# Moving two of ScalarE's four rows in each middle tile to VectorE, in a row normalization

## Chip, cores, metric

The kernel runs on one core of a Trainium2 chip. Times are device microseconds (us). A run is timed several times in turn with the kernel before on the same chip. The span of a profile, from the first to the last instruction, is some 1.7 us shorter than the time.

## The reference

```python
# x: float32, 32 x 512 x 1024
sums = np.sum(np.abs(x), axis=-1, keepdims=True)
return (x / (sums + 1e-8)).astype(np.float32)
```

There are 16384 rows of 1024 numbers. Each is read once and written once, 67.1 MB each way.

## The kernel before

Each of the 128 partitions holds 128 rows, cut into ten tiles of 12 rows and a last one of 8. A tile is loaded by SyncE's queue, reduced on VectorE, scaled in place by VectorE (the first `kv` rows, one instruction) and by ScalarE (the other rows, one instruction each), and stored from ScalarE's queue. Four tile buffers go round: the load of a tile waits until the store four tiles earlier has landed.

```python
R = 12; BUFS = 4
# ...
def normalize(x_tile, r0, k, kv):
    # s = sum |x| by row (line 51), s += EPS (58), inv = 1/s (60), all on VectorE
    nc.vector.tensor_mul(out=x_tile[:, r0:r0+kv, :], in0=x_tile[:, r0:r0+kv, :],     # line 61
                         in1=inv[:, :kv].unsqueeze(2).to_broadcast([P, kv, d]))
    for r in range(kv, k):                                                           # line 68
        nc.scalar.activation(out=row, in_=row, func=Copy, scale=inv[:, r:r+1])
# ...
for i, k in enumerate(rows):
    nc.sync.dma_start(out=x_tile[:, :k, :], in_=piece(x_flat, i))                    # line 78
    normalize(x_tile, 0, k, k - k // 3 - (i == 0))
    nc.scalar.dma_start(out=piece(out_flat, i), in_=x_tile[:, :k, :])                # line 81
```

(The excerpt is tightened; some lines and arguments are cut.)

## Time and profile before

| quantity | before |
|---|---|
| time, median of 3 runs | 317.16 us (316.67 to 318.14) |
| VectorE / ScalarE busy | 234.7 us (74%) / 47.2 us (15%) |
| moved by DMA | 134.2 MB, 425 GB/s over the span |
| share of the 16 DMA engines | load queue 49.8%, store queue 49.1% |
| VectorE waiting for loads | 59.8 us, of which 17.7 us for the first |

### The profile page before, as it was taken

How to read it: one execution, taken by the hardware profiler on the slowest of the kernel's cores; microseconds unless marked ns; L12 is line 12 of the kernel's file. 1: busy time of each engine (PE TensorE's matmuls, PEld its weight loads, DVE VectorE, ACT ScalarE, POOL GpSimd, SP SyncE). 2: the span in 40 equal slices, each digit the busy share in tenths (PEclk: the TensorE clock that was granted, in tenths of full speed). 3: DMA queues.
4: the chain of work that ended last, by engine and by line, in shares of the span. 5: the costliest groups of instructions: out<-in, count | busy, mean ns of one | idle time of the engine just before them, and what ended most of it. 6: DMA issues, size and time to landing. Idle time of an engine off the chain costs nothing.

```text
span 315.5 us, 206 instructions
## 1 busy us (share of the span) xinstructions
DVE 234.7 (74%) x44; ACT 47.2 (15%) x44; POOL 0.2 (0%) x4
## 2 busy tenths in 40 slices
DVE  0079999999999399929955992899199659979500
ACT  0010603105005001300500050013004000502000
POOL 0000000000000000000000000000000000000000
DMA  8999999999999999999999999999999999999996
GB/s 330 467 399 430 467 343 455 399 467 430 399 467 430 399 486 411 405 486 405 424 474 399 436 461 399 467 430 399 467 425 405 474 403 459 407 472 411 424 432 274
DMA packets 3169, 134.23 MB, mean 425 GB/s; under 512 B 352, under 2 KB 352, under 8 KB 352
## 3 DMA queue, kind: packets, MB, share of 16 engines
q1 hardware_dynamic: 1584, 67.11, 49.8%
q10 hardware_dynamic: 1584, 67.11, 49.1%
q14 instruction: 1, 0.01, 0.0%
HBM read 67.11 MB, written 67.11 MB: 425 GB/s over the span
## 4 chain that ended last, share of the span: by engine, by line
another core or an unknown queue 36%; DMA 31%; DVE 26%; SPq 0%; issue 0%; DVEq 0%; ACTq 0%
DMA x_tile<-in_x_dram 16%; DMA out_dram<-x_tile 15%; DVE s L51 15%; DVE x_tile L61 10%; SPq L78 0%; DVE inv L60 0%; DVE s L58 0%; DVEq L60 0%; ACTq L81 0%
## 5 line engine op out<-in xcount | busy, mean ns | idle before, releaser
L51 DVE TENSOR_REDUCE s<-x_tile 128x12 f32<-128x12288 f32 (+1 forms) x11 | 138.2, 12563 | 59.8 <-DMA x_tile<-in_x_dram 59.8
L61 DVE TENSOR_TENSOR x_tile<-x_tile,inv 128x8192 f32<-128x8192 f32 (+2 forms) x11 | 92.4, 8401 | 0.4
L68 ACT ACTIVATE x_tile<-x_tile,inv 128x1024 f32<-128x1024 f32 x43 | 45.9, 1136 | 226.9 <-DVE inv L60 226.9
L68 ACT ACT_TABLE_LOAD x1 | 1.3, 1283 | 17.7 <-DMA x_tile<-in_x_dram 17.7
L60 DVE RECIPROCAL inv<-s 128x12 f32<-128x12 f32 (+1 forms) x11 | 2.5, 226 | 0.9
L58 DVE TENSOR_SCALAR s<-s 128x12 f32<-128x12 f32 (+1 forms) x11 | 1.9, 173 | 0.4
L96 POOL MEMSET const-bfloat16-1.0<- 128x1 bf16 x1 | 0.1, 102 | 0.0
L96 POOL MEMSET const-uint8-127<- 128x1 uint8 x1 | 0.1, 102 | 0.0
L96 POOL MEMSET const-float32-0.0<- 128x1 f32 x1 | 0.1, 99 | 0.2 <-issue 0.2
L96 POOL MEMSET const-float32-1.0<- 128x1 f32 x1 | 0.1, 99 | 0.0
## 6 DMA issues: line engine op xcount, KB each, us to landing
x_tile<-in_x_dram SPq DMA_DIRECT2D x10, 6144.0 KB, 37.6
out_dram<-x_tile ACTq DMA_DIRECT2D x10, 6144.0 KB, 50.7
x_tile<-in_x_dram SPq DMA_DIRECT2D x1, 4096.0 KB, 32.3
out_dram<-x_tile ACTq DMA_DIRECT2D x1, 4096.0 KB, 18.2
```

The source lines that it names most:

```text
L51: nc.vector.tensor_reduce(out=s[:, :k], in_=x_tile[:, r0 : r0 + k, :], axis=mybir.AxisListType.X, op=mybir.AluOpType.add, apply_absolute_v ...
L58: nc.vector.tensor_scalar_add(out=s[:, :k], in0=s[:, :k], scalar1=EPS)
L60: nc.vector.reciprocal(out=inv[:, :k], in_=s[:, :k])
L61: nc.vector.tensor_mul(out=x_tile[:, r0 : r0 + kv, :], in0=x_tile[:, r0 : r0 + kv, :], in1=inv[:, :kv].unsqueeze(2).to_broadcast([P, kv, d]),)
L68: nc.scalar.activation(out=row, in_=row, func=mybir.ActivationFunctionType.Copy, scale=inv[:, r : r + 1],)
L96: nc = _bacc.Bacc("TRN2", target_bir_lowering=False, num_devices=1)
```

## The change

The intent is to divide the scaling differently: two rows of each tile on ScalarE, five of the first one, the others on VectorE.

```diff
-            normalize(x_tile, 0, k, k - k // 3 - (i == 0))
+            normalize(x_tile, 0, k, k - (2 if i else 5))
```

## The prediction

> **What bounds the kernel now.** I read the page first, then the chain that ended last, then the groups with their shapes kept apart, then the timeline, and last a table of stretches. The page's busy lines and its DMA lines:
>
> ```profile
> DVE 234.7 (74%) x44; ACT 47.2 (15%) x44; POOL 0.2 (0%) x4
> ...
> DVE  0079999999999399929955992899199659979500
> ...
> DMA  8999999999999999999999999999999999999996
> ```
>
> VectorE is busy 74% of the span, but the DMA row is at 9 from the second slice to the last but one: the 16 DMA engines never stop. Whoever has spare time, it is not they. The stretches from one load's landing to the next say how close to full they are (columns: stretch and its length, VectorE, ScalarE and GpSimd busy, TensorE clock, DMA share, GB/s):
>
> ```profile
> 111.17:140.20 29.03, 22.05 (x4) 4.26 (x4) 0.00 (x0) 1.00 1.00 433
> 140.20:169.18 28.98, 22.05 (x5) 4.26 (x4) 0.00 (x0) 1.00 1.00 434
> 169.18:198.19 29.01, 22.04 (x4) 4.26 (x4) 0.00 (x0) 1.00 1.00 434
> ```
>
> One tile of 12 rows takes 29.0 us at a DMA share of 1.00, and VectorE works 22.05 us of it. So VectorE has about 6.9 us to spare in each tile. The timeline shows that spare time as a wait for the load, in brackets:
>
> ```profile
> 96.23 8.69 DVE L61 TENSOR_TENSOR x_tile<-x_tile,inv 128x8192 f32<-128x8192 f32 x1
> ...
> 105.00 0.34 ACTq L81 DMA_DIRECT2D out_dram<-x_tile  x1
> 111.17 12.95 DVE L51 TENSOR_REDUCE s<-x_tile 128x12 f32<-128x12288 f32 x1 [6.26 <-DMA x_tile<-in_x_dram]
> ...
> 124.71 4.26 ACT L68 ACTIVATE x_tile<-x_tile,inv 128x1024 f32<-128x1024 f32 x4 [24.21 <-DVE inv L60]
> 124.71 8.69 DVE L61 TENSOR_TENSOR x_tile<-x_tile,inv 128x8192 f32<-128x8192 f32 x1
> 133.49 0.34 ACTq L81 DMA_DIRECT2D out_dram<-x_tile  x1
> ```
>
> The reader is to see that both halves of a scaling start together at 124.71, that ScalarE is done after 4.26 us and VectorE after 8.69, and that the store goes out when VectorE ends. ScalarE's end decides nothing, while VectorE's end is the moment at which a store is issued. Whether that moment matters is told by the chain of the work that ended last:
>
> ```profile
> 82.95 48.50 DMA out_dram<-x_tile
> 131.44 0.02 issue
> ...
> 131.52 0.33 SPq L78
> 131.85 28.65 another core or an unknown queue
> ...
> 248.08 32.26 DMA x_tile<-in_x_dram
> 280.34 0.02 issue
> 280.36 8.70 DVE s L51
> ```
>
> A load is issued when the store of the tile that held its buffer (four tiles earlier) has landed: the store issued at 82.95 lands at 131.44, and the load follows at 131.52. The store took 48.5 us, yet two transfers of 6.29 MB, in and out, fill only 29.0 us. The rest is queueing behind the store before it. That backlog is what the prediction rests on.
>
> **What the Trainium skill says.** (1) "DMA: Bandwidth & Descriptors", section "Where 436 GB/s comes from", gives a fabric ceiling of 435.2 GB/s. The trace agrees: 433 to 434 GB/s in the middle. (2) The same page, "Queues, rings and completion order", says that each DMA engine takes turns packet by packet between the queues that have work. So while loads and stores both have work queued, neither the order nor the speed depends on when a transfer was put in its queue. The trace agrees as far as it goes: equal bytes each way at 29.0 us a tile. [...] (4) "SBUF — State Buffer", section "Who interferes with whom", says that DMA has ports of its own and does not contend with compute engines. The trace lends it no more than weak support: in the tail 417 GB/s were moved while VectorE worked (280.4 to 296.2) and 416 just after it had stopped (296.3 to 304.8).
>
> **The change, part by part.** The first tile keeps 5 rows on ScalarE and 7 on VectorE (before it was 12/3 + 1 = 5 as well). The last tile of 8 rows keeps 2 and 6. Only the nine tiles between change, from 4 rows on ScalarE and 8 on VectorE to 2 and 10. The order of instructions on each engine is otherwise the same, with 18 activations fewer. The rates come from the groups by shape:
>
> ```profile
> L61 DVE TENSOR_TENSOR x_tile<-x_tile,inv 128x8192 f32<-128x8192 f32 x9 | 78.2, 8693 | 0.3
> ...
> L61 DVE TENSOR_TENSOR x_tile<-x_tile,inv 128x6144 f32<-128x6144 f32 x1 | 6.6, 6558 | 0.0
> ```
>
> - VectorE: two rows, 2048 elements, cost 8693 − 6558 = 2135 ns. The product of 10 rows should take 8693 + 2135 = 10828 ns[...]. Nine of them add 19.2 us: busy 234.7 → 253.9 us, 80% of the span.
> - ScalarE: four rows took 4.26 us and the last tile's two took 2.19, so a tile loses 2.07 us, nine lose 18.6: busy 47.2 → 28.6 us, 9%. It was done 4.4 us before VectorE and will be 8.6 us before it; nothing waits for either.
> - In a middle tile: VectorE 22.05 + 2.14 = 24.2 us against 29.0. The wait for the load shrinks from about 6.8 to about 4.6 us, and stores are issued some 2.1 to 2.3 us later. No new sum is on the path unless the store queue runs dry.
> - In the opening, where VectorE runs four tiles without a wait, delays add up: the second tile's store 2.1 us later, the third's 4.3, the fourth's 6.4 (105.00 → 111.4). The fifth tile's load lands at 111.17, so VectorE takes it about 0.2 us late, and the 6.26 us wait is gone. From there the delay falls back to 2.1 to 2.3.
> - Does the store queue run dry? The first store lands just before 73.52, when SyncE issues the fifth load, and the second store was issued at 60.9: 12.6 us to spare, of which 2.1 go. The third was issued at 82.95, and the second lands at about 102.5 (the sixth load goes out at 102.58): 19.6, of which 4.3 go. The fourth was issued at 105.00 and the third lands at 131.44: 26.4, of which 6.4 go. Later ones have about 27 us, of which 2.3 go. It never runs dry, so each store should land when it did, each load be issued when it was, and each tile arrive when it did.
> - In the tail: the last load lands at 280.34. The ninth changed tile is reduced from 256.18 on; its product should end at 278.40 + 2.14 = 280.54. The last tile's reduce then starts 0.2 us late, and its store is issued at about 296.4 instead of 296.24. Page part 6 has for that store
>
> ```profile
> out_dram<-x_tile ACTq DMA_DIRECT2D x1, 4096.0 KB, 18.2
> ```
>
> and 4.19 MB at 425 GB/s need only 9.9 us. So 8.3 us of backlog lie before it, and 0.2 us of delay is hidden. It should land in 18.0 us instead of 18.2, at the same 314.4.
>
> The sum: 19.2 us of VectorE work added, 18.6 us of ScalarE work removed, on the path 0.0 us. Prediction 317.2 us.
>
> **The rivals.** (a) VectorE becomes the bound. It would need over 29.0 us a tile, and it has 24.2. The opening is the only place where it sets the pace; if those 6.4 us counted in full, the time would be 323.6 (+2.0%). Against it stand the 12 to 26 us of backlog. (b) The later store delays the buffer, so the next load. The chain speaks for it, as loads are issued on stores' landings. If a landing moved with its issue, each lap of four tiles would add about 2.1 us, two to three laps 4 to 6 us: 321 to 323. Against it: a store waits behind others for 10 to 27 us before its own bytes move. (c) DMA moves more slowly while VectorE reads and writes on-chip memory. In stretches where VectorE is idle I find 469 GB/s against 431 during a reduce and 457 during a product. If that is real, 19.2 us more at 457 than at 469 cost about 0.5 us. The stretches always fall on the same phase of a tile and packets are counted whole, so I think little of it; the tail's 417 and 416 speak against. (d) A gain. Fewer instructions stand ahead of the store issue on ScalarE, but the issue waits for VectorE anyway. I find nothing that comes earlier.
>
> **Range and chances.** The three runs of before span 316.67 to 318.14, which is 0.5%; my central case adds nothing, so that scatter is most of the range: 316.3 to 318.5, the upper side a little wider for (c). To be slower by over 2% (323.5) takes (a) or (b) in full, which the backlog excludes unless I misread it: 0.02. Faster by over 2% would mean over 6 us less at a DMA share that is already 1.00: 0.005. Within 2%: 0.975.
>
> **What would show it.** Right: ten-row products of 10.83 us, VectorE at about 254 us and ScalarE near 29; waits of the reduce for a load down from 59.8 to about 41 us in total (17.7 at the start, none at the fifth tile and the last, about 4.6 at the five between); tiles still arriving at 140.2, 169.2, 198.2 and so on at 29.0 us; the last store landing in about 18.0 us. Step by step wrong: if tiles arrive later by 2 us a lap, (b) is right and the backlog was not there; if the fifth tile's load lands 6 us later, (a); if the arrivals are 29.1 us or more apart at a share of 1.00, (c).

## The result

The changed kernel took 317.20 us (median of 6 runs, 316.65 to 317.51), the kernel before 317.32 us in the 6 runs that it has by then. The ratio is 0.9993, with a 95% interval from 0.9975 to 1.001. A ratio here is the mean time of one kernel's fast runs over that of the other's of the same rounds, so it isn't quite the ratio of the medians quoted. Executions over 1.5% slower than the fastest of the same kernel are left out of the means.

The profile page after, its busy lines and DMA line:

```profile
DVE 253.8 (80%) x44; ACT 28.5 (9%) x26; POOL 0.2 (0%) x4
...
DVE  0079999999999999949985995899499959999500
...
DMA  8999999999999999999999999999999999999996
```

VectorE gained 19.1 us and ScalarE lost 18.7, while the DMA row has the same digits as before. The stretches from one tile's reduce to the next (columns as in the prediction):

```profile
111.44:140.46 29.02, 24.18 (x4) 2.19 (x2) 0.00 (x0) 1.00 1.00 434
140.46:169.44 28.98, 24.18 (x4) 2.19 (x2) 0.00 (x0) 1.00 1.00 434
169.44:198.47 29.03, 24.18 (x4) 2.19 (x2) 0.00 (x0) 1.00 1.00 433
```

A tile still takes 29.0 us, with VectorE busy 24.18 us of it instead of 22.05. The timeline shows where the extra 2.13 us went:

```profile
111.44 12.95 DVE L51 TENSOR_REDUCE s<-x_tile 128x12 f32<-128x12288 f32 x1
111.48 0.34 ACTq L81 DMA_DIRECT2D out_dram<-x_tile  x1
...
124.97 10.82 DVE L61 TENSOR_TENSOR x_tile<-x_tile,inv 128x10240 f32<-128x10240 f32 x1
...
135.89 0.34 ACTq L81 DMA_DIRECT2D out_dram<-x_tile  x1
140.46 12.95 DVE L51 TENSOR_REDUCE s<-x_tile 128x12 f32<-128x12288 f32 x1 [4.66 <-DMA x_tile<-in_x_dram]
```

The fourth store is issued at 111.48 instead of 105.00, and VectorE no longer waits for the fifth tile. One tile on, the wait is 4.66 us where it was 6.80. The extra work has been taken out of a wait. The chain that ended last, which now runs through other pieces:

```profile
111.48 49.11 DMA out_dram<-x_tile
160.59 0.02 issue
...
218.67 37.75 DMA x_tile<-in_x_dram
256.42 0.02 issue
256.44 12.96 DVE s L51
...
280.79 8.61 DVE s L51
```

The fourth store was issued 6.5 us later and lands at 160.59; in the kernel before it landed at 160.50, as the load waiting for it shows. That is the backlog at work. VectorE's share of the chain rose from 26% to 42%. In part this is because the last tile's reduce now starts when VectorE is free (280.71), 0.1 us after its load landed (280.60), where before it started at 280.36 on the landing at 280.34: two nearly equal predecessors changed places. For the rest, the chain now runs through the fourth store, issued at 111.48, and no longer through the third, at 82.95, so more of VectorE's opening lies on it. The time did not move. A share of the chain is thus not a measure of what an engine costs.

### The profile page after: what moved, and what is told of

It reads as the page before. It is cut to its first block, busy times and chain, and to the rows that moved or that the text cites. A ratio compares the mean times of both kernels' runs of the same rounds, so it can differ in the third digit from the quotient of the medians.

```text
span 315.7 us, 188 instructions
## 1 busy us (share of the span) xinstructions
DVE 253.8 (80%) x44; ACT 28.5 (9%) x26; POOL 0.2 (0%) x4
## 4 chain that ended last, share of the span: by engine, by line
DVE 42%; DMA 33%; another core or an unknown queue 18%; issue 0%; SPq 0%; DVEq 0%; ACTq 0%
DVE s L51 23%; DVE x_tile L61 18%; DMA x_tile<-in_x_dram 17%; DMA out_dram<-x_tile 16%; DVE inv L60 0%; DVE s L58 0%; SPq L78 0%; DVEq L60 0%; ACTq L81 0%
## 5 line engine op out<-in xcount | busy, mean ns | idle before, releaser
L61 DVE TENSOR_TENSOR x_tile<-x_tile,inv 128x10240 f32<-128x10240 f32 (+2 forms) x11 | 111.6, 10146 | 0.4
L68 ACT ACTIVATE x_tile<-x_tile,inv 128x1024 f32<-128x1024 f32 x25 | 27.2, 1139 | 245.9 <-DVE inv L60 245.9
```

Source lines behind the costliest of these rows:

```text
L61: nc.vector.tensor_mul(out=x_tile[:, r0 : r0 + kv, :], in0=x_tile[:, r0 : r0 + kv, :], in1=inv[:, :kv].unsqueeze(2).to_broadcast([P, kv, d]),)
L68: nc.scalar.activation(out=row, in_=row, func=mybir.ActivationFunctionType.Copy, scale=inv[:, r : r + 1],)
```

## The experiments

Eleven runs were made, in three groups; each group shared its runs of the kernel before, whose median in them was 316.9 to 317.0 us. The theory under test is the backlog: a store issued later still lands at the same time as long as the store queue has work, so nothing behind it moves. The time from a store's issue to the landing of the store in front of it is called its reserve: a delay up to that long is hidden. The rivals are that the delay passes on with the buffers, that DMA slows beside a busy VectorE, and, for the later runs, that only VectorE's pace against 29.0 us counts.

### all_vector: ScalarE scales nothing in the middle tiles

```diff
-            normalize(x_tile, 0, k, k - (2 if i else 5))
+            normalize(x_tile, 0, k, k - ((5, 0)[i > 0] if i < len(rows) - 1 else 2))
```

> VectorE scales all 12 rows of the nine middle tiles, ScalarE none there (first and last tile as before). VectorE then takes 22.05 + 4 x 1.07 = 26.3 us a middle tile against 29.0 of the DMA. Backlog theory (a store is issued later but waits behind earlier stores anyway, so its landing does not move): stores two to four are issued 4.3, 8.5 and 12.8 us later than in the kernel before, against 12.6, 19.6 and 26.4 us to spare; the last store is issued near 298.9, the store ahead of it lands near 304.9, so the time stays at 317.2 (within 0.3%). Rival 'delay passes on' (each lap of the four buffers inherits VectorE's delay): 4.3 us in each of two to three laps, 326 to 330. Rival 'DMA slows beside VectorE': 38 us more VectorE work, 1 us or more, 318.2 upward, with tiles arriving over 29.05 us apart.

Measured: 316.69 us, ratio 0.9975 (0.9928 to 1.0023). VectorE was busy 272.8 us (87%), and tiles arrived at 111.1, 140.1 and 169.1, again 29.0 us apart. Both rivals named so far fall here: 38 us more VectorE work than in the kernel before slowed no transfer, and twice the delay of the change reached nothing. The last store was issued at 298.24 and took 15.6 us to land, against 18.2: the delay is paid out of queueing.

### after_x4, before_x4, after_x8: more VectorE work

An extra reduce into scrap, from rows that are there anyway, in each of the nine middle tiles. It stands ahead of the product, so the store waits for it. The same edit on the kernel before gives before_x4, and 8 rows in place of 4 give after_x8.

```diff
+        if extra:
+            scrap = stats.tile([P, R], FP32)
+            nc.vector.tensor_reduce(out=scrap[:, :extra], in_=x_tile[:, r0 : r0 + extra, :], ...)
...
-            normalize(x_tile, 0, k, k - (2 if i else 5))
+            normalize(x_tile, 0, k, k - (2 if i else 5), 4 if 0 < i < len(rows) - 1 else 0)
```

> The changed kernel, with an extra reduce of 4 rows into scrap on VectorE in each of the nine middle tiles (4096 x 1.042 + 153 ns = 4.42 us), output unchanged. VectorE takes 24.2 + 4.4 = 28.65 us a tile, still under the 29.0 of the DMA. Rival 'only the pace counts' (VectorE is free as long as it is under 29.0 us a tile): 317.2. Backlog theory: VectorE runs back to back from the second tile on and never catches up; stores two to ten are issued at 38.8 + 28.65 n, so the tenth tile's store at 296.6, while the store ahead of it lands at 290.4: the queue is dry there for some 6 us, and the last tile's store is issued at 312.5 and lands near 323; time about 325.6 (324 to 327), with tiles arriving as before until the last load.

> The kernel before, with the same extra reduce of 4 rows (4.42 us) in each middle tile. VectorE takes 22.05 + 4.4 = 26.5 us a tile. This adds VectorE work without taking any from ScalarE. Backlog theory: last tile's store issued near 299, the one ahead lands near 304.9, so 317.2, within 0.3%. 'Delay passes on': 4.4 us a lap, 326 upward. It also tells whether what matters is VectorE's total per tile and not who scales: all_vector has the same total with ScalarE idle.

> The changed kernel with an extra reduce of 8 rows (8.69 us) in each middle tile: VectorE 32.95 us a tile, over the DMA's 29.0, so VectorE is the bound. Backlog theory: VectorE back to back from 38.8 on, tenth tile's store at 38.8 + 9 x 32.95 = 335.3, last store at 351.2, landing near 361.5: time about 364. 'Only the pace counts': nine tiles each (32.95 - 29.0) = 3.95 us longer, 317.2 + 35.6 = 353. The loads' waits on VectorE are gone and DMA share falls under 0.9.

| run | VectorE per middle tile | time, us | ratio (95%) |
|---|---|---|---|
| before_x4 | 26.4 us | 317.32 | 0.9997 (0.9937 to 1.0058) |
| after_x4 | 28.5 us | 325.27 | 1.0245 (1.0196 to 1.0294) |
| after_x8 | 32.8 us | 363.69 | 1.1455 (1.14 to 1.151) |

(The tile times are the spacing of the store issues while VectorE runs without waits.) Once more 26.4 us cost nothing, whoever did the scaling. At 28.5 us VectorE is still faster than the DMA's 29.0, and yet the kernel loses 8.3 us (clear of no change; by the 2% rule its verdict is "unclear", as the interval holds 1.02): a pace under 29.0 us is not enough. The tail shows why. Stretches of after_x4:

```profile
282.20:291.30 9.10, 9.06 (x2) 0.29 (x1) 0.00 (x0) 1.00 0.65 282
291.30:297.50 6.20, 6.20 (x2) 0.00 (x0) 0.00 (x0) 1.00 0.30 127
297.50:311.20 13.70, 13.43 (x4) 2.19 (x2) 0.00 (x0) 1.00 0.93 402
```

The same stretches of the changed kernel:

```profile
282.20:291.30 9.10, 8.93 (x4) 1.36 (x2) 0.00 (x0) 1.00 1.00 432
291.30:297.50 6.20, 5.19 (x1) 0.83 (x1) 0.00 (x0) 1.00 0.91 396
297.50:311.20 13.70, 0.00 (x0) 0.00 (x0) 0.00 (x0) 1.00 1.01 435
```

All loads have landed by then, and in after_x4 the ninth store landed at 291.28 while the tenth was issued only at 295.50. The DMA engines ran dry. At the full 434 GB/s, the bytes missing are worth 9.10 x (432 - 282) / 434 + 6.20 x (396 - 127) / 434 + 13.70 x (435 - 402) / 434 = 3.1 + 3.8 + 1.0 = 8.0 us, of the 8.3 that the run lost. (The last load had landed 1.6 us later, at 282.22, after the sixth, seventh and eighth loads had come 29.4 to 29.5 us apart; I have no cause for that. It is not part of the 8.0 us: by 282.2 us the packets of this run and of the changed kernel had moved nearly the same, 120.6 and 120.7 MB.) The expectation had put the tenth store at 296.6, the landing ahead of it at 290.4 and the time at 325.6.

In after_x8 VectorE is the bound: the last store was issued at 349.59 (351.2 expected) and the time was 363.7 (364 expected), 11 us above what counting pace alone gives.

### early_x4 and late_x4: the same extra work in one half only

```diff
-  4 if 0 < i < len(rows) - 1 else 0
+  4 if 0 < i < 6 else 0                  # early_x4: tiles two to six
+  4 if 5 < i < len(rows) - 1 else 0      # late_x4: tiles seven to ten
```

> after_x4 cost 8.3 us (325.3 against 316.9) though VectorE stayed at 28.5 us a tile. Here the extra reduce is in the second to the sixth tile alone. Backlog theory: at the sixth tile VectorE is as late as in after_x4, but the four tiles after it take 24.2 us each against 29.0 and it catches up; the tenth tile's store is issued near 282, 8 us before the store ahead of it lands: 317 (within 0.5%), none of the 8.3 us. Rival 'the cost is spread evenly, a share for each tile with extra work': 5/9 of 8.3, so 321.5.

> The extra reduce in the seventh to the tenth tile alone. Backlog theory: VectorE enters the seventh tile on time (169.4) and takes 28.5 us a tile against arrivals 29.0 apart, so the tenth tile's store is issued near 285, 5 us before the one ahead lands; the last store near 300.6, 4 us before the one ahead: 317 (within 0.5%). Rival 'even share': 4/9 of 8.3, 320.6. Rival 'only the end of the kernel counts, work near the tail is on the path': the whole 4.4 us of the tenth tile or more, 321 upward. Early and late together make up after_x4: if both cost nothing, costs do not add, and it was the lateness carried from the opening to the tail that counted.

Measured: early_x4 317.52 us, ratio 1.0023 (1.0001 to 1.0045); late_x4 317.65 us, ratio 1.0025 (1.0007 to 1.0043). Together the two edits are after_x4, which cost 8.3 us; apart each costs 0.7 to 0.8 us by the ratios, and at most 1.4 by the ends of the intervals. How long their last store took, early_x4 first, by the DMA issues of the two pages:

```profile
out_dram<-x_tile ACTq DMA_DIRECT2D x1, 4096.0 KB, 17.7
```

```profile
out_dram<-x_tile ACTq DMA_DIRECT2D x1, 4096.0 KB, 13.5
```

In early_x4 the delay is gone by the end, as VectorE caught up. In late_x4 the store was issued at 301.08, 4.8 us later than in the kernel before, and had that much less queue ahead of it. In the two profiles the last store landed at 314.41 and 314.55, against 314.39 before. So neither an even share nor nearness to the tail explains the cost. What fits is lateness carried from the opening to a point where no store is left in front. The 0.2% by which both ratios lie above 1 isn't to be seen in these profiles and stays unexplained.

A plainer account fits as well. In after_x4 VectorE waits for a load once, for the first:

```profile
DVE s L51 <- DMA x_tile<-in_x_dram: 17.7, 1, 17.7
```

So VectorE is the bound of that run, and its time is a sum: the first load landed at 17.67, VectorE worked on until the last store was issued at 311.19 (291.8 us busy and 1.7 us of small gaps), and that store, with none in front of it, took 11.1 us, to 322.30. For the changed kernel the same sum would be 17.7 + 253.8 + 1.7 + 11.1 = 284.3 us, 30.3 us before its last store landed (314.56). The extra reduces raised VectorE's busy time by 38.0 us in after_x4, by 21.0 in early_x4 and by 17.2 in late_x4. Only 38.0 is more than 30.3, and the difference of 7.7 us is what the last landing moved. So the total of VectorE's work against the slack of the whole kernel explains the three runs too, and no run here separates it from lateness carried to the tail. More extra work, in the late tiles alone, might.

### scalar_less: ScalarE's part of the change alone

```diff
-        for r in range(kv, k):
+        for r in range(kv, k - unscaled):    # unscaled = 2 in the nine middle tiles
```

> One part of the change alone: the kernel before, with two of ScalarE's four rows of each middle tile left unscaled (wrong on purpose), VectorE's eight rows as before. ScalarE loses the 18.6 us of busy time that it loses in the change, VectorE gets nothing. Backlog theory and my prediction: 0.0 us, 317 within 0.3%, since ScalarE's scaling ends 4.4 us before VectorE's and nothing waits for it. Rival 'ScalarE's time hinders its issuing of stores': earlier stores, and some 1 us faster.

Measured: 317.21 us, ratio 1.0009 (0.9988 to 1.003), ScalarE busy 28.5 us; the result was wrong, as intended. The saving on ScalarE is worth nothing by itself.

### dma_only: the transfers with no work between

```diff
-            normalize(x_tile, 0, k, k - k // 3 - (i == 0))
```

> Loads and stores of the kernel before with no work between (the output is the input, wrong on purpose): the floor of the transfers with these tiles, queues and buffers. At 434 GB/s 134.2 MB take 309.3 us; with some 2.4 us until the first bytes of the first load arrive and 1 to 3 us around the span: 313 to 317. So at most 1.3% is to be had by any division of the scaling. If it were under 311, the division of work would cost something that I have not seen, and the backlog theory would be incomplete.

Measured: 316.66 us, ratio 0.9983 (0.9931 to 1.0034). Its output is wrong, which doesn't matter for the time. Without any reduce or scaling the same loads and stores take the same time. It is also the plainest test of DMA beside VectorE: from 30 to 300 us the DMA engines move 433 GB/s here, with VectorE idle, and 431 and 432 in the kernel before and in all_vector. Both kernels stand at this time, so with these tiles, queues and buffers I expect no division of the rows between engines to beat them by more than the scatter.

### before_b3, after_b3, all_vector_b3: three tile buffers

```diff
-    BUFS = 4
+    BUFS = 3
```

> The kernel before with three tile buffers in place of four: the load of a tile is issued when the store three tiles earlier has landed, so less can queue. Backlog theory, with one queue each way sharing 434 GB/s worked through by hand: with three buffers the store queue is nearly empty when a store is issued, loads can no longer be issued ahead, and some us of DMA time are lost: about 319.8 (318.5 to 321). Rival 'stores are hidden whatever the depth': 317.

> The changed kernel with three buffers. Backlog theory: with the reserve gone, VectorE's extra 2.1 us a tile now shows; three laps of three tiles would give up to 6.4, the queue model worked by hand gives 323.1, so 3.3 us above the kernel before with three buffers (accepted: 1.5 to 6.5). Rival 'VectorE's time below 29.0 us a tile never shows' (DMA at its ceiling whatever the buffers): no difference between the two with three buffers, within 0.3%.

> All 12 rows of the middle tiles on VectorE, three buffers. Backlog theory: a further 2.1 us a tile, 325.2 by the same working, 5 us above the kernel before with three buffers (accepted: 3 to 13). With four buffers the same division of the rows cost nothing (316.7 against 316.9). Rival as above: no difference.

| run | time, us | ratio (95%) | VectorE waiting for loads |
|---|---|---|---|
| before_b3 | 331.36 | 1.042 (1.0353 to 1.0486) | 82.5 us |
| after_b3 | 329.76 | 1.0369 (1.0307 to 1.0431) | 59.8 us |
| all_vector_b3 | 330.12 (330.68 with the slow run) | 1.0409 (1.0346 to 1.0471) | 42.0 us |

These expectations failed twice. The level of before_b3 is 11.6 us above the 319.8 that the queue model gave, and the order that was to show the vanished reserve isn't there: the intervals overlap, and a difference of some 2 us either way couldn't be seen. The differences expected could have been: after_b3 was to be 3.3 us slower than before_b3 (at least 1.5) and all_vector_b3 some 5 (at least 3), and by the means of the fast runs they were 2.1 and 0.8 us faster. The rival of the expectation, no difference, is nearer. VectorE's added work came out of its waits here too (82.5 - 59.8 = 22.7 us, for 19.3 us added). The stretch from 30 to 300 us, first of before_b3, then of the kernel before:

```profile
30.00:300.00 270.00, 203.88 (x40) 43.70 (x41) 0.00 (x0) 1.00 0.99 412
```

```profile
30.00:300.00 270.00, 222.41 (x44) 45.88 (x43) 0.00 (x0) 1.00 1.00 431
```

With three buffers the DMA engines count as busy for the same share but move 412 GB/s instead of 431. In the trace the 16 engines' completion marks for one transfer lie up to 11.3 us apart in before_b3, and never over 3.0 us in the kernel before. My model shared one rate between two queues and had no engines that drift apart. That the drift causes the lower rate isn't shown, and after_b3 speaks against it: 415 GB/s in the same stretch, with marks never over 3.7 us apart. What the traces do show is that single packets took longer. The packets of 49152 bytes took 1.815 us in the median in both kernels, but 3% of the loads' packets took over 1.9 us in the kernel before, and 15% in before_b3. What such slow packets, of loads and stores, took beyond 1.815 us adds up to 1.9 and 10.8 us for each of the 16 engines. Why they took longer stays open. That the loss with three buffers hides the effect of the division is a guess; another is that a later store leaves more of the DMA to the load in flight. So these runs neither confirm the backlog theory nor tell against it for four buffers.

## Why the prediction was right

- **The bound.** The prediction read the DMA as full at 29.0 us a tile. dma_only shows it directly: 316.66 us with no work on the compute engines.
- **The sizes.** Ten-row products were to take 10.83 us and took 10.82 to 10.83; VectorE was to be busy 253.9 us and was 253.8; ScalarE 28.6, and was 28.5. The waits of the reduce for a load were to fall from 59.8 to about 41 us, and fell to 41.0, with none at the fifth tile and the last, and 4.62 to 4.68 us at the five between.
- **The opening.** The fourth store was to be issued 6.4 us late, at 111.4; it went out at 111.48, and its landing moved by under 0.1 us. The sums of delay against time to spare were the right comparison, but one of them was misread: "later ones have about 27 us" holds for the fifth to the eighth store. The ninth had 23.8 us (249.48 to 273.32) and the tenth 11.8 (278.48 to 290.27). The change's 2.4 us fits into that too; after_x4, which issued its tenth store 17 us later than the kernel before, found the gap there and paid.
- **The tail.** The last store was to be issued near 296.4 and to land in 18.0 us at 314.4. It was issued at 296.58, took 18.0 and landed at 314.56. About 0.2 us more than predicted is in this profile from the start: the last load landed at 280.60 instead of 280.34, and the first tile began 0.08 us later. The 9.9 us for a last store with nothing in front of it were too few: in after_x4 it took 11.1.
- **Rival (a), VectorE as the bound,** was said to need over 29.0 us a tile; after_x8 is that case. For eleven tiles that condition was wrong: at 28.5 us VectorE already is the bound, since the first load and the last store stand outside its work. An estimate from the sum above puts the condition at 24.2 + 30.3 / 9 = 27.5 us for each middle tile; runs were made at 26.4 (free) and 28.5 (not) only.
- **Rival (b), the delay passed on with the buffer,** fell in the profile after, whose landings stay within 0.4 us, and in all_vector with twice the delay. With three buffers I expected it to appear, and no run showed it.
- **Rival (c), slower DMA beside VectorE,** fell in all_vector and dma_only. The 469 and 431 GB/s were an effect of the stretches chosen, as the prediction suspected.
- **Rival (d), a gain from a freer ScalarE,** fell in scalar_less.

## What to carry to other kernels

When the transfers are full, ask of a delayed store not how late it is but whether another store is still in front of it. Add up an engine's lateness through the opening, and compare it with the smallest reserve, which is at the tail: work that is free in either half can cost 8 us in both. Check the plain sum as well, first load, all work of the engine, last store: in after_x4 it gave the time. Before tuning how work is divided between engines, run the transfers alone; here that run took as long as the kernels, so nothing was left to gain from dividing.

## What the Trainium skill lacked or had wrong

- "DMA: Bandwidth & Descriptors", section "Where 436 GB/s comes from", says that for transfers between HBM and SBUF the HBM side, about 358 GB/s, binds, and names no condition there. One core running alone moved 433 to 434 GB/s from and to HBM for most of this kernel, at the 435 that the same section gives for the fabric. Elsewhere the page gives 358 GB/s as what is left to a core when both cores of a pair stream, so the sentence lacks that condition; no run here has two cores.
- "DMA: Bandwidth & Descriptors", section "Queues, rings and completion order", says that the engines take turns by packet, but not that unequal packets then get unequal shares. The last load, of 8 rows (packets of 32768 bytes in the trace), ran beside stores of 12 rows (packets of 49152 bytes): its 4.19 MB took 24.2 us after the load before it (256.16 to 280.34), or 173 GB/s, 40% of 434; and 32768 / (32768 + 49152) is 40%. In dma_only it took 24.2 us too (277.75 to 301.93). Only this pair of sizes was tried.
- None of the pages I read says that fewer buffers lower the DMA rate at an unchanged busy share: 412 GB/s at a share of 0.99 with three buffers, 431 at 1.00 with four, because single packets took longer.
